# Block products of an MLP down-projection: their weights prepared in three parts, and one weight chunk of the last stage scheduled sooner

## The chip, the cores and the metric

The kernel runs on one core of a Trainium2 chip. The metric is the device time of one execution in microseconds (us), as the median of several executions. A profile is one execution recorded by the hardware. Its engines are TensorE (PE: matmuls; PEld: its weight loads), VectorE (DVE), ScalarE (ACT), GpSimd (POOL) and SyncE (SP, which only issues DMAs here). Each engine works through its own queue of instructions in order, and semaphores make one engine wait for another.

## The reference

Two layers of a decoder trunk over 512 tokens and 1024 features, all in float32. Each layer has a mixer (attention and convolution in layer 0, gated linear attention in layer 1), a gated MLP with a short convolution, and a gated per-layer embedding:

```python
def _conv_ffn(h, w_up, conv_w, conv_b, w_down):
    u = _causal_depthwise_conv(h @ w_up, conv_w) + conv_b
    gate, up = jnp.split(u, 2, axis=-1)
    return (jax.nn.gelu(gate, approximate=False) * up) @ w_down

def _per_layer_embedding(x, p_i, norm, w_gate, w_proj):
    gate = jax.nn.sigmoid(_rms_norm(x, norm) @ w_gate)
    return gate * (p_i @ w_proj)
...
        x = x + _conv_ffn(_rms_norm(x, ffn_norm[i]), ffn_w_up[i], ffn_conv_w[i], ffn_conv_b[i], ffn_w_down[i])
        x = x + _per_layer_embedding(x, p[i], ple_norm[i], ple_w_gate[i], ple_w_proj[i])
```

`w_down` is 2816 x 1024 per layer. This change touches the product with it, in both layers, and the last stage, which is the per-layer embedding of layer 1.

## The kernel before

**Three matmuls for one.** Every float32 operand is split into a high part (a rounded copy, made by ACT: `wh` of a weight) and a low part (the rest, made by DVE: `wl = raw - wh`). A product is then three matmuls: high by high, high by low, low by high. So each chunk of weights passes through ACT and then DVE before PE can use it. Lines 138 and 139 do this for ordinary weights, 811 and 812 (`cut_blocks`) for the weights of block products, 1335 and 1336 (`chunk`) in the last stage.

**Block products.** A part of the weights is multiplied by Strassen's scheme in Winograd's form: seven products of half-sized blocks in place of eight. It needs sums and differences of the four weight blocks b11, b12, b21, b22, which `seven_forms` makes in place with four DVE subtractions (lines 831, 832, 834, 836), and of the activations. From the blocks come four sets of split weights: `plain` (before any subtraction), `t13` (after the first two subtractions, a full chunk from `ev`), `t2` (after the third, half a chunk) and `last` (after the fourth, made in `seven` itself). `seven` is a generator: each `next` emits one group of products. The first is `plain` by tokens into W, which ACT copies into the two result banks X and Y (lines 865 and 866). The second group begins with `t13` into V, then a `plain` and a `t2` product; the third and fourth use `t13` and `last`. V is added to both halves of the odd output row at the end (line 1237, the V add).

**The down-projection.** `down` works on four units of 256 output columns. Rows A and B of `w_down` are multiplied in the ordinary way, in steps listed in `plan`; rows C, the last eight row blocks, by `seven`, for units 0 to 3 in layer 0 and 0 to 2 in layer 1. A plan entry with a fifth number s carries the block products of unit s interleaved with its own steps. Units 0 and 2 have their C weights in a `raw` tile; units 1 and 3 in two `zt` tiles, loaded as even and odd row blocks, whose `plain` set is made in two halves (lines 102 and 103).

**What sets the order.** PE's order is the order of the program text. DVE's and ACT's are set by a scheduler from the order of the text and its priorities. The split weights `wh` and `wl` have three buffers each. The list `todo` holds the work that needs such buffers, each with the number it needs; `pump(n)` says that n more have come free and takes from the list what fits. An ordinary cut needs one; the preparation of a unit needed two, for `plain` and `t13` together.

**The last stage.** `ple1` multiplies a gate matrix by the same kind of scheme, with PE, DVE and ACT in the written order from line 1418 on. Ahead of that stand two chunks of block (0,0) (`w11`), the subtraction `minus(b11, b12, b11)` in two halves, and `wt1`, the split of its first half, which is the third chunk. `wt1` is used by the s1 products. Between the first six matmuls of these and the rest stand eight sums of squares (line 324) and eight transposes (line 1262); then come the s2 products, transposes (1364) and the projection (lines 158 to 160, with the chunk `wj`).

Of the kernel before, what the change touches and what calls it, by code (L numbers as in the profile page):

```python
# [14 lines left out]
ALU = mybir.AluOpType  # L15
# [42 lines left out]
class Kernel:  # L58
# [758 lines left out]
    def seven_forms(self, ev, od, raw=None):  # L817


        nc = self.nc  # L820
        b11, b12, b21, b22 = ev[:, :, :P], ev[:, :, P:], od[:, :, :P], od[:, :, P:]
        if raw is not None:
            plain = self.cut_blocks(raw[:, :, :P])
        else:
            h, l = (self.wp.tile([P, 1024], F32R, tag=g, name=self.nm(g), bufs=3) for g in ("wh", "wl"))
            h, l = (x.rearrange("p (j u n) -> p j u n", u=2, n=P) for x in (h, l))
            for u, b in enumerate((b11, b21)):
                self.split((h[:, :, u], l[:, :, u]), b)
            plain = lambda j, c: (h[:, j, c], l[:, j, c])

        nc.vector.tensor_tensor(b11, b12, b11, ALU.subtract)
        nc.vector.tensor_tensor(b12, b22, b12, ALU.subtract)  # L832
        t13 = self.cut_blocks(ev)
        nc.vector.tensor_tensor(b11, b22, b11, ALU.subtract)
        t2 = self.cut_blocks(b11, False)
        nc.vector.tensor_tensor(b21, b21, b11, ALU.subtract)
        return plain, t13, t2

    def seven(self, od, ws, xg, forms, keep=True):

# [249 lines left out]
    def down(self, i, acts, forms, both, work, finish):  # L1090


        nc, tc = self.nc, self.tc
        H = S // 2
        wd = self.a["ffn_w_down"][i].rearrange("(k p) n -> p k n", p=P)
        rows = {"A": (8, 14), "B": (0, 8), "C": (14, 22)}

        plan = [(0, "A", 0, 3), (0, "A", 3, 6), (0, "B", 0, 4), (0, "B", 4, 8)]
        plan += [(1, "A", 0, 3), (1, "A", 3, 6), (1, "B", 0, 4), (1, "B", 4, 8, 0)]
        plan += [(2, "B", 0, 4, 1), (2, "B", 4, 8, 2)]  # L1100
        if i == 0:
            plan += [(2, "A", 0, 4, 3), (2, "A", 4, 6), (3, "B", 0, 4), (3, "B", 4, 8), (3, "A", 0, 3), (3, "A", 3, 6)]
            loads = ["A0", "B0", "A1", "B1", "C0", "B2", "C2", "A2", "B3", "A3"]
            inner = ["C1", "C3"]
        else:
            plan += [(2, "A", 0, 3), (2, "A", 3, 6), (3, "B", 0, 4), (3, "B", 4, 8)]
            plan += [(3, "C", 0, 4), (3, "C", 4, 8), (3, "A", 0, 3), (3, "A", 3, 6)]
            loads = ["A0", "B0", "A1", "B1", "C0", "B2", "C2", "A2", "B3", "C3", "A3"]
            inner = ["C1"]
        blocked = 4 - i  # L1110
        plan = [p if len(p) == 5 else p + (None,) for p in plan]
        got, cuts, gens = {}, {}, {}

        def cols(u):
            return slice(2 * P * u, 2 * P * u + 2 * P)

        def load(key):
            k0, k1 = rows[key[0]]
            u = int(key[1])
            raw = self.raw(k1 - k0, 2 * P)  # L1120
            nc.sync.dma_start(raw, wd[:, k0:k1, cols(u)])
            got[key] = (raw, None)

        def load_inner(key):
            k0, k1 = rows[key[0]]
            u = int(key[1])
            parts = []
            for q in range(2):
                t = both().rearrange("p a (b n) -> p (a b) n", n=2 * P)
                nc.sync.dma_start(t, wd[:, k0 + q : k1 : 2, cols(u)])  # L1130
                parts.append(t)
            got[key] = (None, parts)

        def cut(t):
            u, name, k0, k1, _ = plan[t]
            cuts[t] = self.cut(got[f"{name}{u}"][0][:, k0:k1], "a")
            if k1 == rows[name][1] - rows[name][0] and loads:
                load(loads.pop(0))

        def prepare(u):  # L1140
            raw, parts = got[f"C{u}"]
            ev, od = parts or self.by_parity(raw)
            ws = self.seven_forms(ev, od, raw)
            gens[u] = self.seven(od, ws, acts[14:], forms, False)

        def cut_done(u):

            raw, _ = got[f"C{u}"]
            if raw is not None and loads:
                load(loads.pop(0))  # L1150
            elif raw is None and inner:
                load_inner(inner.pop(0))

        todo = []
        for t, p in enumerate(plan):
            todo.append((1, lambda t=t: cut(t)))
            if p[4] is not None:
                todo.append((2, lambda u=p[4]: prepare(u)))
        free = 3

        def pump(n):
            nonlocal free
            free += n
            while todo and todo[0][0] <= free:
                need, f = todo.pop(0)
                free -= need
                f()

        def add(m, ps):
            nc.vector.tensor_tensor(self.xT[m], self.xT[m], ps, ALU.add)  # L1170

        due = [2 if u < blocked else 1 for u in range(4)]
        block_left = blocked
        next_unit = 0

        banks = {}
        with tc.manual_schedule(engines={ET.PE}):
            with tc.high_priority(offset=300):
                for _ in range(2):
                    load(loads.pop(0))  # L1180
                pump(0)
            for t, (u, name, k0, k1, s) in enumerate(plan):
                own = u not in banks
                if own:
                    banks[u] = [self.ps(), self.ps()]
                ends = t + 1 == len(plan) or plan[t + 1][0] != u
                joined = i == 0 and u == 3

                def steps(lo, hi):
                    for k in range(lo, hi):  # L1190
                        for c in range(2):
                            self.mm3(
                                banks[u][c], cuts[t](k, c * P, (c + 1) * P), acts[rows[name][0] + k0 + k],
                                start=own and k == 0, stop=ends and k == k1 - k0 - 1, skip_group_check=joined,
                            )

                def settled(ends):
                    nonlocal next_unit
                    if ends:
                        for c in range(2):  # L1200
                            add(2 * u + c, banks[u][c])
                        due[u] -= 1
                    while not block_left and next_unit < 4 and not due[next_unit]:
                        for m in (2 * next_unit, 2 * next_unit + 1):
                            finish(m)
                        next_unit += 1

                if s is None:
                    steps(0, k1 - k0)
                    settled(ends)  # L1210
                    pump(1)
                    if work:
                        work.pop(0)()
                        if not work:
                            load_inner(inner.pop(0))
                else:
                    g = gens[s]
                    steps(0, 1)
                    next(g)
                    steps(1, 2)  # L1220
                    next(g)
                    steps(2, 3)
                    next(g)
                    cut_done(s)
                    pump(1)
                    steps(3, 4)
                    settled(ends)
                    pump(1)
                    X, Y, V = next(g)
                    if i == 0 and s == 3:  # L1230
                        banks[3] = [X, Y]
                    else:
                        add(2 * s, X)
                        add(2 * s + 1, Y)
                    pump(1)
                    x = self.xT[2 * s + 1].rearrange("p (u t) -> p u t", u=2)
                    nc.vector.tensor_tensor(x, x, V.unsqueeze(1).to_broadcast([P, 2, H]), ALU.add)
                    due[s] -= 1
                    block_left -= 1
                    settled(False)  # L1240
# [69 lines left out]
    def ple1(self, fp):  # L1310
# [31 lines left out]
        def minus(out, x, y):  # L1342
            for q in range(2):
                c = slice(2 * q, 2 * q + 2)
                nc.vector.tensor_tensor(out[:, c, :], x[:, c, :], y[:, c, :], ALU.subtract)
# [65 lines left out]
        proj_load(1)  # L1411
        b21 = block(1, 0, False)
        proj_load(0)
        minus(b11, b12, b11)
        wt1 = [chunk(b11[:, :2, :])]
        X, Q = [[self.ps() for _ in range(2)] for _ in range(2)]
        both = (0, H)
        with tc.manual_schedule(engines={ET.PE, ET.DVE, ET.Activation}):
# [525 lines left out]
```

## Time and profile before

| | us |
|---|---|
| median of 3 runs | 1243.28 (1241.5 to 1243.61) |
| the profiled execution | 1243.01 |
| its span, first to last instruction | 1241.2 |
| PE busy | 1225.9 |
| DVE busy | 920.4 |
| ACT busy | 640.2 |

In a row of the timeline the columns are start and duration in us, engine, line, operation, output and inputs, shape, and count. In square brackets stands the idle time of the engine ahead of the instruction and what ended it. Matmuls overlap in their durations, so the work of PE is read from start to start: a 512-column matmul follows the one before it after about 0.23 us. The down-projection of layer 0 runs from 419 to 538 us, that of layer 1 up to 1176 us, and the last stage from there to the end.

### The profile page before, as it was taken

The page shows a single profiled execution, that of the slowest core. Times are in us where ns is not written, and L with a number is a line of the kernel's source. Part 1 is how long each engine was busy: PE and PEld are TensorE (multiplying, and loading weights), DVE is VectorE, ACT ScalarE, POOL GpSimd, SP SyncE. Part 2 cuts the span into 40 slices and gives each one's busy share as a digit, 9 for nine tenths or more (in the row PEclk, how much of TensorE's full clock was granted, in tenths as well). Part 3 has the DMA queues.
Part 4 walks back from the last instruction along what each step waited for, and adds up shares of the span by engine and source line. Part 5 has one row for each costly group of instructions (what it writes and reads, how often), then busy time and mean ns, then how long its engine had stood idle before and what let it go on. Part 6 is the DMA issues. An engine that isn't in the chain of part 4 may idle for free.

```text
span 1241.2 us, 16978 instructions
## 1 busy us (share of the span) xinstructions
PE 1225.9 (99%) x6740; PEld 1047.2 (84%) x6740; DVE 920.4 (74%) x1449; ACT 640.2 (52%) x1036; POOL 42.7 (3%) x64
## 2 busy tenths in 40 slices
PE   9999999999999999999999999999999999999998
PEld 8877788889999888888978888888889999888877
DVE  6886556987878976745779875559878789968575
ACT  7466343554556743544563544435455557635354
POOL 3500000000000000000100000000000000000000
PEclk9999999999999999999999999999999999999989
DMA  6322232224242432233322212333322423413501
GB/s 215 102 71 61 79 102 79 92 68 136 69 135 70 136 117 68 88 102 100 108 69 68 76 61 70 100 110 102 102 77 69 136 68 128 139 57 117 173 1 68
DMA packets 111060, 117.56 MB, mean 95 GB/s; under 512 B 2777, under 2 KB 106259, under 8 KB 110981
## 3 DMA queue, kind: packets, MB, share of 16 engines
q1 hardware_dynamic: 109616, 115.35, 28.5%
q8 instruction: 53, 0.87, 0.3%
q0 software_dynamic: 560, 0.42, 0.3%
q10 hardware_dynamic: 804, 0.70, 0.2%
q14 instruction: 27, 0.21, 0.1%
HBM read 114.37 MB, written 2.10 MB: 94 GB/s over the span
## 4 chain that ended last, share of the span: by engine, by line
PE 87%; DVE 8%; ACT 3%; issue 2%; POOL 1%; ACTq 0%; DVEq 0%; POOLq 0%
PE ps L158 16%; PE ps L159 16%; PE ps L160 16%; PE pa L159 5%; PE pa L158 5%; PE pa L160 5%; PE ps L854 4%; PE ps L856 4%; PE ps L855 4%; PE pa L856 2%; PE pa L855 2%; PE pa L854 2%; DVE wl L139 1%; PE ps L1357 1%; PE ps L1358 1%
## 5 line engine op out<-in xcount | busy, mean ns | idle before, releaser
L138 ACT ACTIVATE wh<-raw 128x1024 fp32r<-128x1024 f32 (+4 forms) x170 | 169.3, 998 | 225.4 <-PE ps L159 167.9
L139 DVE TENSOR_TENSOR wl<-raw,wh 128x1024 fp32r<-128x1024 f32 (+4 forms) x170 | 194.9, 1147 | 94.6 <-ACT wh L138 94.2
L158 PE MATMUL ps<-a,wh 128*128 128x512 f32 x416 | 162.7, 391 | 0.0
L159 PE MATMUL ps<-a,wh 128*128 128x512 f32 x416 | 162.3, 390 | 0.0
L160 PE MATMUL ps<-a,wl 128*128 128x512 f32 x416 | 162.0, 390 | 0.0
L158 PE MATMUL ps<-b,wh 128*128 128x512 f32 x320 | 126.2, 396 | 0.5 <-ACT b L102 0.5
L160 PE MATMUL ps<-b,wl 128*128 128x512 f32 x320 | 125.7, 393 | 0.0
L159 PE MATMUL ps<-b,wh 128*128 128x512 f32 x320 | 125.2, 392 | 0.0
L811 ACT ACTIVATE wh<-raw 128x1024 fp32r<-128x1024 f32 x54 | 57.1, 1058 | 69.1 <-DVE raw L832 30.1
L158 PEld LDWEIGHTS ps<-a,wh 128*128 128x128 f32 x416 | 78.1, 188 | 16.6 <-issue 0.7
L160 PEld LDWEIGHTS ps<-a,wl 128*128 128x128 f32 x416 | 78.1, 188 | 16.4
L159 PEld LDWEIGHTS ps<-a,wh 128*128 128x128 f32 x416 | 78.2, 188 | 16.2 <-issue 0.3
L158 PE MATMUL pa<-a,wh 128*128 128x512 f32 x224 | 87.8, 392 | 0.0
L159 PE MATMUL pa<-a,wh 128*128 128x512 f32 x224 | 87.8, 392 | 0.0
L160 PE MATMUL pa<-a,wl 128*128 128x512 f32 x224 | 87.1, 389 | 0.0
L812 DVE TENSOR_TENSOR wl<-raw,wh 128x1024 fp32r<-128x1024 f32 x54 | 65.9, 1221 | 28.0 <-ACT wh L811 27.9
L158 PEld LDWEIGHTS ps<-b,wh 128*128 128x128 f32 x320 | 60.1, 188 | 13.5 <-ACT b L102 1.3
L910 DVE SCALAR_TENSOR_TENSOR zt<-z,vfa,zt 128x511 f32<-128x511 f32 (+1 forms) x92 | 67.1, 746 | 5.3 <-ACT zt L908 5.0
L160 PEld LDWEIGHTS ps<-b,wl 128*128 128x128 f32 x320 | 60.1, 188 | 12.7
L159 PEld LDWEIGHTS ps<-b,wh 128*128 128x128 f32 x320 | 60.2, 188 | 11.5
L160 PEld LDWEIGHTS pa<-a,wl 128*128 128x128 f32 x224 | 42.1, 188 | 9.2
L158 PEld LDWEIGHTS pa<-a,wh 128*128 128x128 f32 x224 | 42.3, 189 | 7.3
(460 smaller groups left out, 2945.1 us busy)
## 6 DMA issues: line engine op xcount, KB each, us to landing
raw<-in_ffn_w_up_dram SPq DMA_DIRECT2D x44, 1024.0 KB, 4.9
raw<-in_ffn_w_down_dram SPq DMA_DIRECT2D x13, 1024.0 KB, 5.2
raw<-in_hy_w_in_dram SPq DMA_DIRECT2D x8, 1024.0 KB, 5.0
raw<-in_gla_w_in_dram SPq DMA_DIRECT2D x8, 1024.0 KB, 5.1
raw<-in_ffn_w_down_dram SPq DMA_DIRECT2D x8, 768.0 KB, 4.3
raw<-in_ple_w_gate_dram SPq DMA_DIRECT2D x6, 1024.0 KB, 5.0
raw<-in_gla_w_out_dram SPq DMA_DIRECT2D x4, 1024.0 KB, 4.9
zt<-in_ffn_w_down_dram SPq DMA_DIRECT2D x6, 512.0 KB, 3.7
```

The lines of the kernel that those rows point to most:

```text
L138: nc.scalar.activation(hv, v, AF.Copy)
L139: nc.vector.tensor_tensor(lv, v, hv.bitcast(F32), ALU.subtract)
L158: mm(out, lh, rh, start=start, stop=False, **kw)
L159: mm(out, lh, rl, start=False, stop=False, **kw)
L160: mm(out, ll, rh, start=False, stop=stop, **kw)
L811: nc.scalar.activation(h, src, AF.Copy)
L812: nc.vector.tensor_tensor(l, src, h.bitcast(F32), ALU.subtract)
L854: mm(out, wh, xh, start=first and j == 0, stop=False, **kw)
L855: mm(out, wh, xl, start=False, stop=False, **kw)
L856: mm(out, wl, xh, start=False, stop=j == ND // 2 - 1, **kw)
L910: nc.vector.scalar_tensor_tensor(out=y[:, tap:], in0=z[:, : S - tap], scalar=w[:, f : f + 1], in1=y[:, tap:], op0=ALU.mult, op1=ALU.add,)
L1357: mm(o, lh, rl, start=False, stop=False, **kw)
```

## The change

The preparation of a unit is cut into three. `first_forms` makes `plain` and does the first two subtractions, as soon as one buffer is free. `more_forms` of `down` makes `t13` as soon as the next is free. The rest (third and fourth subtraction and `t2`) is put on a list `pending`, which is worked off after the adds of a unit. In the main loop one `pump(1)` moves ahead of `settled(ends)`, and the V add moves ahead of the adds of X and Y. In `ple1` the subtraction and the third chunk get a higher priority.

```diff
     def seven_forms(self, ev, od, raw=None):
+        plain = self.first_forms(ev, od, raw)
+        return plain, self.cut_blocks(ev), self.more_forms(ev, od)
+
+    def first_forms(self, ev, od, raw=None):
...
         nc.vector.tensor_tensor(b11, b12, b11, ALU.subtract)
         nc.vector.tensor_tensor(b12, b22, b12, ALU.subtract)
-        t13 = self.cut_blocks(ev)
+        return plain
+
+    def more_forms(self, ev, od):
+        nc = self.nc
+        b11, b21, b22 = ev[:, :, :P], od[:, :, :P], od[:, :, P:]
         nc.vector.tensor_tensor(b11, b22, b11, ALU.subtract)
         t2 = self.cut_blocks(b11, False)
         nc.vector.tensor_tensor(b21, b21, b11, ALU.subtract)
-        return plain, t13, t2
+        return t2
...
+        def pend():
+            while pending:
+                pending.pop(0)()
...
-        def prepare(u):
+        def first_forms(u):
             raw, parts = got[f"C{u}"]
             ev, od = parts or self.by_parity(raw)
-            ws = self.seven_forms(ev, od, raw)
-            gens[u] = self.seven(od, ws, acts[14:], forms, False)
+            gens[u] = ev, od, self.first_forms(ev, od, raw)
+
+        def more_forms(u):
+            ev, od, plain = gens[u]
+            t13 = self.cut_blocks(ev)
+
+            def rest():
+                gens[u] = self.seven(od, (plain, t13, self.more_forms(ev, od)), acts[14:], forms, False)
+
+            pending.append(rest)
...
             if p[4] is not None:
-                todo.append((2, lambda u=p[4]: prepare(u)))
+                todo.append((1, lambda u=p[4]: first_forms(u)))
+                todo.append((1, lambda u=p[4]: more_forms(u)))
...
                     steps(0, k1 - k0)
                     settled(ends)
                     pump(1)
+                    pend()
...
                     steps(3, 4)
+                    pump(1)
                     settled(ends)
+                    X, Y, V = next(g)
                     pump(1)
-                    X, Y, V = next(g)
+                    x = self.xT[2 * s + 1].rearrange("p (u t) -> p u t", u=2)
+                    nc.vector.tensor_tensor(x, x, V.unsqueeze(1).to_broadcast([P, 2, H]), ALU.add)
                     if i == 0 and s == 3:
                         banks[3] = [X, Y]
                     else:
                         add(2 * s, X)
                         add(2 * s + 1, Y)
-                    pump(1)
-                    x = self.xT[2 * s + 1].rearrange("p (u t) -> p u t", u=2)
-                    nc.vector.tensor_tensor(x, x, V.unsqueeze(1).to_broadcast([P, 2, H]), ALU.add)
+                    pend()
...
         proj_load(0)
-        minus(b11, b12, b11)
-        wt1 = [chunk(b11[:, :2, :])]
+        with tc.high_priority(offset=150):
+            minus(b11, b12, b11)
+            wt1 = [chunk(b11[:, :2, :])]
```

More of the change, by code (lines that the diff above doesn't have):

```diff
@@ L1111, in down @@
         plan = [p if len(p) == 5 else p + (None,) for p in plan]
-        got, cuts, gens = {}, {}, {}
+        got, cuts, gens, pending = {}, {}, {}, []
+        def pend():
+            while pending:
+                pending.pop(0)()
         def cols(u):
```

## The prediction

> **What bounds the kernel now.** I read the page's shares first, then the slices, then the waits of the matmul engine, and last the timelines of the stages that the diff touches.
>
> ```profile
> span 1241.2 us, 16978 instructions
> PE 1225.9 (99%) x6740; PEld 1047.2 (84%) x6740; DVE 920.4 (74%) x1449; ACT 640.2 (52%) x1036; POOL 42.7 (3%) x64
> PEclk9999999999999999999999999999999999999989
> ```
>
> TensorE is the bound from end to end. So the change can gain only what TensorE loses now: idle time in front of matmuls, and time at a lower clock. All slices show 9 for the granted clock except the last but one. The waits of PE in the whole span name the lines of this change:
>
> ```profile
> PE ps L1357 <- DVE wl L1336: 2.2, 1, 2.2
> PE pa L856 <- DVE wl L812: 1.5, 2, 0.8
> PE pa L854 <- ACT wh L811: 0.7, 2, 0.4
> ```
>
> Columns are total us, times, and the longest. The first is the largest single wait of PE in the kernel: one wait of 2.2 us in the last stage. The other two are the block products of the down-projection: two waits each, one in each layer's down-projection. The clock goes with the first one:
>
> ```profile
> 1185.30:1192.10 6.80, 6.80 (x26) 6.02 (x25) 3.99 (x6) 3.95 (x6) 1.01 (x1) 0.50 0.00 0
> ```
>
> This is the view by stretches; the third figure from the end is the granted clock, 0.50 for 6.8 us.
>
> **The change, part by part.** Three things move; the instructions stay the same in number and kind (one merged pair of DVE subtractions is now split in order). The orders of DMA issues on SP, of POOL, and of PE's products are as before, so no transfer and no product is moved.
>
> *1. The t13 weights of unit 1 (both layers).* PE in the first down-projection:
>
> ```profile
> 471.48 0.39 PE L160 MATMUL ps<-b,wl 128*128 128x512 f32 x1
> 472.23 0.39 PE L854 MATMUL pa<-a,wh 128*128 128x256 f32 x1 [0.36 <-ACT wh L811]
> 472.45 0.28 PE L855 MATMUL pa<-a,wh 128*128 128x256 f32 x1
> 473.49 0.38 PE L856 MATMUL pa<-a,wl 128*128 128x256 f32 x1 [0.75 <-DVE wl L812]
> 473.71 0.28 PE L854 MATMUL pa<-a,wh 128*128 128x256 f32 x1
> 473.83 0.28 PE L855 MATMUL pa<-a,wh 128*128 128x256 f32 x1
> ```
>
> ```profile
> 465.64 1.38 DVE L1170 TENSOR_TENSOR xT<-xT,ps 128x512 f32<-128x512 f32 x2
> 468.90 0.69 DVE L831 TENSOR_TENSOR zt<-zt 128x512 f32<-128x512 f32 x1
> 469.51 0.68 DVE L1237 TENSOR_TENSOR xT<-xT,pa 128x512 f32<-128x512 f32 x1
> 470.10 0.69 DVE L832 TENSOR_TENSOR zt<-zt,zt 128x512 f32<-128x512 f32 x1
> 472.21 1.23 DVE L812 TENSOR_TENSOR wl<-zt,wh 128x1024 fp32r<-128x1024 f32 x1 [1.42 <-ACT wh L811]
> 477.44 1.23 DVE L812 TENSOR_TENSOR wl<-zt,wh 128x1024 fp32r<-128x1024 f32 x1 [1.88 <-ACT wh L811]
> 470.57 0.36 ACT L865 COPY ps<-pa 128x256 f32<-128x256 f32 x1 [1.52 <-PE pa L856]
> 471.10 1.07 ACT L811 ACTIVATE wh<-zt 128x1024 fp32r<-128x1024 f32 x1
> ```
>
> A 256-wide matmul starts 0.12 us after the one before (473.71 to 473.83); a 512-wide one takes 0.23 (below). So the loss at this place is 0.75 - 0.23 = 0.52 in front of wh, 1.04 - 0.12 = 0.92 in front of wl, and 0.10 twice where the first matmul after a wait spaces 0.22: 1.64 us. The cause stands on DVE and ACT. Between 465.64 and the second subtraction (470.10) DVE runs eight half-width steps, 0.60 apart: two adds, half of plain, an add, the other half, subtraction, V add, subtraction. Then ACT does its square and the two copies out of PSUM, which wait for PE until 470.57, and only then wh.
>
> In the new order five steps are left: two halves of plain, subtraction, one add, subtraction. The second subtraction starts at 465.64 + 4 x 0.60 = 468.04 and ends at 468.73. ACT takes wh next, ahead of the square and the copies: 468.8 to 469.9. DVE does two adds meanwhile and then wl, 470.0 to 471.2. PE wants wh at 471.48 + 0.23 = 471.71 and wl 0.24 later at 471.95. Both are there, wl with 0.75 to spare, and ACT is done with wh before the copies' PE product ends at 470.57, so they are not held. Gain 1.64 here. The waits view counts two of each wait with equal longest values, so the second layer's unit 1 is taken as the same: 3.28 together. Bounds: 0 where wl comes no sooner, 3.28 where it comes in time; I take 3.28, since the margin of 0.75 is more than one DVE step.
>
> The V add goes to after t2 and before the last chunk's wl. That wl has 1.88 us of DVE idle ahead of it (477.44), which covers one step of 0.60; without that cover it would cost those 0.60 in each unit's last product. The rest (t2 and the second pair of subtractions) falls behind the adds, but t2 feeds the fourth product, 24 matmuls of 0.12 behind the first of t13: 2.9 us later. Units 0, 2 and 3 show no such wait on PE now, and there only the V add changes its place: 0.
>
> *2. The third chunk of the last stage.*
>
> ```profile
> 1175.88 1.06 ACT L1335 ACTIVATE four<-raw 128x1024 fp32r<-128x1024 f32 x1 [2.55 <-DVE raw L1345]
> 1179.94 1.04 ACT L1335 ACTIVATE wh<-raw 128x1024 fp32r<-128x1024 f32 x1
> 1177.17 1.22 DVE L1336 TENSOR_TENSOR four<-raw,four 128x1024 fp32r<-128x1024 f32 x1
> 1178.41 0.43 DVE L103 TENSOR_TENSOR b<-zt,b 128x256 fp32r<-128x256 f32 x1
> 1181.30 0.69 DVE L280 TENSOR_TENSOR acc<-acc,sq 128x512 f32<-128x512 f32 x1
> 1183.11 1.23 DVE L1336 TENSOR_TENSOR wl<-raw,wh 128x1024 fp32r<-128x1024 f32 x1
> ```
>
> ```profile
> 1181.81 0.39 PE L1356 MATMUL ps<-wh,a 128*128 128x512 f32 x1
> 1184.39 0.50 PE L1357 MATMUL ps<-wl,a 128*128 128x512 f32 x1 [2.19 <-DVE wl L1336]
> 1185.91 1.70 PE L324 MATMUL pa<-ones,acc 128*128 128x1 f32 x8
> 1194.72 0.39 PE L1356 MATMUL ps<-four,a 128*128 128x512 f32 x1
> 1197.45 1.04 PE L1364 MATMUL pa<-cf,xT 128*128 128x128 f32 x8
> 1198.24 0.47 PE L1356 MATMUL ps<-four,b 128*128 128x512 f32 x1
> 1201.32 0.39 PE L159 MATMUL pa<-wl,four 128*128 128x512 f32 x1
> 542.28 1.05 PE L324 MATMUL pa<-ones,acc 128*128 128x1 f32 x8
> 543.20 0.48 PE L158 MATMUL ps<-a,wh 128*128 128x512 f32 x1
> ```
>
> ACT's conversion goes from 1179.94 to right behind the one at 1175.88, so 1176.84 to 1177.9; DVE's goes from 1183.11 to right behind 1177.17, so 1178.3 to 1179.5. PE wants wl at 1181.81 + 0.23 = 1182.04: the wait goes. What DVE and ACT did in between comes 1.1 us later. The low part of the last pair (1178.41) ends at about 1179.9; PE wants that pair six matmuls ahead of 1181.81, at 1180.45. The sum of squares ended at 1181.30 + 0.69 = 1181.99; it goes to 1182.8, since one subtraction of 0.3 now stands behind it. PE wants it six matmuls after 1181.81, at 1183.17: covered, by 0.4 us alone.
>
> From 1181.81 to the s2 products at 1194.72 are 12.91 us. At full clock and without a wait: 24 matmuls at (1197.45 - 1194.72)/12 = 0.2275, so 5.46; eight sums at 543.20 - 542.28 = 0.92; eight transposes at 1198.24 - 1197.45 = 0.79; 0.08 for the slower start behind them. That is 7.25, a gain of 5.66: 2.45 of it is the wait with its slower start, 3.2 is the half clock.
>
> That the half clock goes too is my choice. It is the only one inside the span's stages, it begins 0.9 us after the only wait over 2 us ends, and the 1.6 us lost in the down-projections, spread over two waits, brought none. Bounds: 2.45 (the clock dip stays) and 5.66.
>
> *3. What is late next.* PE comes sooner to the projection, whose weight chunk wj is behind a long DVE chain:
>
> ```profile
> 1187.64 0.16 DVE L167 TENSOR_SCALAR rs<-pa 128x4 f32<-128x4 f32 x1 [0.92 <-PE pa L324]
> 1189.70 2.36 DVE L1336 TENSOR_TENSOR four<-raw,four 128x1024 fp32r<-128x1024 f32 x2 [1.90 <-ACT four L1335]
> 1196.50 2.36 DVE L1336 TENSOR_TENSOR wl<-raw,wh 128x1024 fp32r<-128x1024 f32 x2 [0.97 <-ACT wh L1335]
> 1198.78 1.22 DVE L1336 TENSOR_TENSOR wl<-four,wh 128x1024 fp32r<-128x1024 f32 x1
> ```
>
> wj's wl ends at 1200.00. Moving the third chunk ahead takes nothing off this chain, it only reorders it; sooner it gets by its idle time, 0.92 + 1.90 + 0.97 = 3.79, all of it behind PE or behind ACT copies that wait for PE. If all goes, wj is there at 1196.2; PE wants it at 1201.32 - 5.66 = 1195.66. A new wait of 0.55, with its restart 0.65. Bounds: 0, and 4.4 where none of the idle time goes. I take 0.65, since all three waits end with PE work that comes 2.5 us or more sooner. Gain of the stage: 5.0.
>
> **Sum.** 3.28 + 5.0 = 8.3 us. The profiled execution took 1243.01 us (1.8 beside its span), 0.27 under the median 1243.28 of the runs shown. 1243.0 - 8.3 = 1234.7.
>
> [...]
>
> **The rivals.**
>
> The clock dip stays, for it comes from the eight sums and eight transposes (some 1.7 us of thin work on PE), or moves to another place. For it: that thin work stays and follows more closely. Against: the eight sums at 542.28 brought no dip, and the clock fell at 1185.3, ahead of the sums at 1185.91. PE then reaches wj late enough for no wait: gain 3.28 + 2.45 = 5.7, time 1237.3.
>
> wj does not come sooner, and takes the place of the wait removed. For it: DVE is full in this stretch. Against: the three idle stretches above. Gain 3.28 + 5.66 - 4.4 = 4.5: 1238.5.
>
> The change does not do what it says for unit 1: wl comes late still, for instance because wh finds no free buffer. Against: the buffer it gets was last read by unit 0's last product, over before wh's new start. Gain 5.0 alone: 1238.0.
>
> The new order costs the five units that do not wait now. At 1.2 us in each, 6 of the 8.3 are gone: 1241, no measurable change. For it: every unit's V add is moved. Against: the 1.88 us of idle DVE time.
>
> Slower: a clock that does not recover. If the thin work that now follows closely lets the clock fall and it stays at 0.50, each us at half clock costs 0.5. To end 2.5 us above 1243 it must take 10.8 us back, 22 us at half clock from the sums on, three times the dip seen: 1246. Against: the clock came back at 1192 under ordinary matmuls.
>
> **How the numbers follow.** Forecast 0.60, own range 1233.2 to 1236; dip stays 0.16; wj late 0.08; unit 1 unhelped 0.06; five units hurt 0.06; clock lost 0.04. The low end is the sum without the wj wait (1234.1) less about 1 us, since the three runs shown lie 2.1 us apart. The high end 1239.0 takes in the first three rivals. 0.2% (2.5 us) is about what can be told from no change: faster 0.90, same 0.06, slower 0.04.
>
> **What would show it.** In the waits of PE: no DVE wl of the last stage's s1 products, no wh and wl of t13 in the pa products; granted clock 1.00 from the start of the last stage to its final products; the eight sums in about 0.9 us; a short new PE wait (about 0.5) in front of the projection for wj. I am wrong if PE waits for acc at the sums, if a stretch at 0.50 is left there, or if DVE's V add shows up as what a last chunk waits for.

## The result, and the profile after

The changed kernel takes 1234.78 us (median of 6 runs, 1234.57 to 1235.43). The kernel before, in the 6 runs beside it, takes 1241.83 (1240.62 to 1243.61). The ratio is 0.9943, with a 95% interval of 0.993 to 0.9955. The profiled execution took 1235.43 us, 7.58 less than the profiled one of before.

The page of the changed kernel, its span, busy time and granted clock in 40 slices:

```profile
span 1233.7 us, 16975 instructions
PE 1222.7 (99%) x6740; PEld 1045.2 (85%) x6740; DVE 920.2 (75%) x1449; ACT 640.7 (52%) x1036; POOL 43.6 (4%) x64
PEclk9999999999999999999999999999999999999999
```

The work is the same; the 8 in the clock's last slice but one is gone. The waits of PE in the whole span (total us, times, longest):

```profile
PE pa L1649 <- DVE F L1647: 1.5, 2, 1.0
PE pa L1723 <- ACT qT L1715: 1.3, 2, 0.7
PE pa L193 <- DVE mhalf L182: 1.3, 1, 1.3
PE pa L600 <- ACT pT L654: 1.0, 1, 1.0
PE ps L158 <- ACT b L102: 0.5, 1, 0.5
PE pa L159 <- DVE wl L139: 0.2, 1, 0.2
PE pa L1780 <- ACT vt L1544: 0.2, 1, 0.2
```

These seven stood in the view of before too. The three that named the lines of the change are gone, and no new one is long enough to appear. (Lines have moved: 811 and 812 keep their numbers, the V add is 1255, the block products 863 to 865, the last stage's chunks 1359 and 1360, its products 1380 to 1382.)

Where the time went is read from PE instructions that both programs have, the first of them the first transposes of the kernel. Before:

```profile
9.10 1.04 PE L478 MATMUL ps<-cf,xin 128*128 128x128 f32 x8
464.17 0.39 PE L160 MATMUL ps<-b,wl 128*128 128x512 f32 x1
1203.81 0.39 PE L1356 MATMUL ps<-wh,a 128*128 128x512 f32 x1
```

After:

```profile
10.05 1.04 PE L478 MATMUL ps<-cf,xin 128*128 128x128 f32 x8
465.17 0.39 PE L160 MATMUL ps<-b,wl 128*128 128x512 f32 x1
541.75 1.05 PE L324 MATMUL pa<-ones,acc 128*128 128x1 f32 x8
1179.57 0.39 PE L1380 MATMUL ps<-wh,a 128*128 128x512 f32 x1
1196.24 0.39 PE L1380 MATMUL ps<-wh,a 128*128 128x512 f32 x1
```

The other two starts of before stand in the prediction: eight sums at 542.28 and first s1 product at 1181.81. They give:

| stretch | before | after | gain |
|---|---|---|---|
| up to unit 1 of layer 0's down-projection | 464.17 | 465.17 | -1.00 |
| from there to the eight sums of layer 0's last stage | 78.11 | 76.58 | 1.53 |
| from there to the s1 products of layer 1's last stage | 639.53 | 637.82 | 1.71 |
| s1 products to s3 products | 22.00 | 16.67 | 5.33 |

The gains add up to 8.57. The execution profiled after began 1.0 us later, which leaves 7.57. 0.95 of it is there at the first transposes, long before the change; the kernel of the third experiment, which is that of before up to the last stage, reaches that stage 0.8 us later than the profiled execution of before (1182.61 in a row below, against 1181.81). So this offset belongs to the execution. The traces show where it comes from. The list of clock stretches has the first one at full clock begin 4.32 us after the first instruction in the profiled execution of before and 7.04 in that after the change; for the third experiment it is an estimate, about 7.5, since its eight 512-column matmuls from 6.44 us on take 2.40 where those of after take 2.19 from 6.43 on. Ahead of that rise the first 512-column matmuls start about 0.44 us apart, later 0.23. The later the rise in these three, the later the first transposes: 9.10, 10.05 and 10.27 us.

The down-projection of layer 0, DVE and ACT around unit 1's `t13`:

```profile
469.05 0.69 DVE L836 TENSOR_TENSOR zt<-zt,zt 128x512 f32<-128x512 f32 x1
470.93 1.23 DVE L812 TENSOR_TENSOR wl<-zt,wh 128x1024 fp32r<-128x1024 f32 x1
474.44 0.69 DVE L1255 TENSOR_TENSOR xT<-xT,pa 128x512 f32<-128x512 f32 x1 [0.17 <-PE pa L865]
476.91 1.22 DVE L812 TENSOR_TENSOR wl<-zt,wh 128x1024 fp32r<-128x1024 f32 x1 [1.77 <-ACT wh L811]
```

```profile
469.83 1.06 ACT L811 ACTIVATE wh<-zt 128x1024 fp32r<-128x1024 f32 x1 [3.28 <-DVE zt L836]
471.62 0.36 ACT L874 COPY ps<-pa 128x256 f32<-128x256 f32 x1 [0.21 <-PE pa L865]
```

and PE there:

```profile
472.58 0.39 PE L160 MATMUL ps<-b,wl 128*128 128x512 f32 x1
472.81 0.28 PE L863 MATMUL pa<-a,wh 128*128 128x256 f32 x1
472.93 0.28 PE L864 MATMUL pa<-a,wh 128*128 128x256 f32 x1
473.04 0.28 PE L865 MATMUL pa<-a,wl 128*128 128x256 f32 x1
```

ACT takes `wh` before the copies out of PSUM, not behind them, and PE goes into the block products without a gap.

The last stage on PE:

```profile
1180.93 0.95 PE L324 MATMUL pa<-ones,acc 128*128 128x1 f32 x8
1181.74 1.07 PE L1286 MATMUL pa<-cf,pin 128*128 128x128 f32 x8
1186.76 0.39 PE L1380 MATMUL ps<-four,a 128*128 128x512 f32 x1
1193.10 0.39 PE L158 MATMUL pa<-wh,four 128*128 128x512 f32 x1
1193.61 0.50 PE L159 MATMUL pa<-wl,four 128*128 128x512 f32 x1
1193.95 0.40 PE L160 MATMUL pa<-wh,four 128*128 128x512 f32 x1
```

and on DVE, the third chunk (first row), the sum of squares that PE needs, and the chain to `wj` (last row):

```profile
1176.07 1.22 DVE L1360 TENSOR_TENSOR wl<-raw,wh 128x1024 fp32r<-128x1024 f32 x1
1179.76 0.68 DVE L280 TENSOR_TENSOR acc<-acc,sq 128x512 f32<-128x512 f32 x1
1184.24 2.37 DVE L1360 TENSOR_TENSOR four<-raw,four 128x1024 fp32r<-128x1024 f32 x2
1190.06 2.36 DVE L1360 TENSOR_TENSOR wl<-raw,wh 128x1024 fp32r<-128x1024 f32 x2
1192.34 1.22 DVE L1360 TENSOR_TENSOR wl<-four,wh 128x1024 fp32r<-128x1024 f32 x1
```

The brackets with idle time that stood in these rows of before are gone: from the third chunk to `wj` DVE runs without a stop. By stretches (the third figure from the end is the granted clock), from the s1 products to the s2 products and on:

```profile
1179.50:1186.80 7.30, 7.30 (x43) 6.29 (x42) 7.30 (x12) 5.81 (x9) 1.85 (x1) 1.00 0.00 0
1186.80:1200.00 13.20, 13.07 (x62) 10.61 (x61) 11.67 (x12) 8.93 (x13) 0.00 (x0) 1.00 0.01 1
```

One more thing has to be known to read the runs. Executions of the kernel before differ in their mean granted clock, and the time follows it. The 29 beside the first four experiments fall into three groups: 1.000 (6 runs, 1240.5 to 1241.0 us), 0.998 (10 runs, 1241.7 to 1242.7) and 0.997 (13 runs, 1242.9 to 1243.7). The profiled one, at 0.997, has 6.8 us at half clock, which is 0.5 x 6.8 / 1241 = 0.003 of the span. Half that stretch is 0.0014. So the groups are read as no, one and two such halves; of two the profile of before is the example, of one that of the first experiment below. By this the dip is there in most executions and not in all.

### The profile page after: what moved, and what is told of

The parts are those of the page before. It is cut to its first block, busy times and chain, and to the rows that moved or that the text cites. A ratio compares the mean times of both kernels' runs of the same rounds, so it can differ in the third digit from the quotient of the medians.

```text
span 1233.7 us, 16975 instructions
## 1 busy us (share of the span) xinstructions
PE 1222.7 (99%) x6740; PEld 1045.2 (85%) x6740; DVE 920.2 (75%) x1449; ACT 640.7 (52%) x1036; POOL 43.6 (4%) x64
## 4 chain that ended last, share of the span: by engine, by line
PE 86%; DVE 9%; ACT 2%; issue 2%; POOL 1%; DMA 0%; ACTq 0%; DVEq 0%; POOLq 0%
PE ps L158 16%; PE ps L159 16%; PE ps L160 16%; PE pa L159 5%; PE pa L158 5%; PE pa L160 5%; PE ps L863 4%; PE ps L865 4%; PE ps L864 4%; PE pa L865 2%; PE pa L864 2%; PE pa L863 2%; DVE wl L139 1%; PE ps L1382 1%; PE ps L1381 1%
```

## The experiments

**The down-projection alone.** The changed kernel with the last part taken back:

```diff
-        with tc.high_priority(offset=150):
-            minus(b11, b12, b11)
-            wt1 = [chunk(b11[:, :2, :])]
+        minus(b11, b12, b11)
+        wt1 = [chunk(b11[:, :2, :])]
```

> The change without its part in the last stage. Theory (the two parts add up, each removes its own waits of PE): the waits for t13 in the pa products are gone in both layers, the 2.2 us wait for wl and the half clock of 6.8 us stay; 3.1 us faster than before (0.25%). Rival (the gain hangs on the phase of the clock, not on the waits): the half clock goes here too, since everything comes 3 us sooner; 6 us or more faster.

Measured: 1239.58 us (11 runs, 1237.57 to 1240.11) against 1242.30 for the 29 of before, ratio 0.9975 (0.9966 to 0.9984). Groups of equal mean clock compare better: 1237.6 against 1240.5 to 1241.0 at 1.000, 1238.4 to 1238.8 against 1241.7 to 1242.7 at 0.998, 1239.6 to 1240.1 against 1242.9 to 1243.7 at 0.997. Between the middle runs of these groups lie 3.1, 3.4 and 3.3 us, and 3.28 was predicted. The waits for `t13` are gone, the wait of the last stage stays, and behind it the half clock, about 3.4 us long this time:

```profile
PE ps L1381 <- DVE wl L1360: 2.2, 1, 2.2
```

```profile
1178.00:1183.00 5.00, 2.82 (x14) 2.00 (x12) 4.97 (x8) 1.36 (x3) 0.00 (x0) 1.00 0.00 0
1183.00:1186.40 3.40, 3.40 (x19) 3.30 (x18) 1.28 (x3) 2.15 (x4) 1.01 (x1) 0.57 0.00 0
1186.40:1200.00 13.60, 13.60 (x65) 11.29 (x64) 10.69 (x11) 9.98 (x14) 0.00 (x0) 0.98 0.00 1
```

The length is an estimate from these rows and from matmul starts: a mean clock of 0.57 over 3.40 us is 2.9 us at 0.50, and these are the last of them, from about 1183.5; and the starts at 1186.25, 1186.67, 1187.00 and 1187.23 are 0.42, 0.33 and 0.23 apart, so it is back at about 1186.9.

**The last stage alone.** The kernel before with only that part:

```diff
-        minus(b11, b12, b11)
-        wt1 = [chunk(b11[:, :2, :])]
+        with tc.high_priority(offset=150):
+            minus(b11, b12, b11)
+            wt1 = [chunk(b11[:, :2, :])]
```

> The last stage's part alone. Theory: the waits for t13 stay (1.5 and 0.7 us), the 2.2 us wait and the half clock are gone, a wait of about 0.3 us for the projection's chunk comes; 5.2 us faster than before in an execution that had the half clock. Rival (the half clock comes from the sums and transposes): the clock still falls, only 2.4 us faster.

Measured: 1238.28 (7 runs, 1237.75 to 1239.53), ratio 0.9969 (0.9959 to 0.998). All seven have a mean clock of 0.999 or more, and no half clock shows in the profiled one's last stage. Against before's runs at 0.997 (middle 1243.2) that is 4.9 less, where 5.0 was predicted; against those at 1.000 (middle 1240.7) it is 2.5. The waits of the block products are still in its view:

```profile
PE pa L856 <- DVE wl L812: 1.5, 2, 0.8
PE pa L854 <- ACT wh L811: 0.7, 2, 0.4
```

The two halves gain 2.7 and 4.0 in medians, 6.7 together. The whole change gains 7.05 against the six runs of before beside it, and 7.5 against these 29. With runs of before that spread over 3 us, this shows no sign that the halves disturb each other.

**Is it the idle time, or the thin work?** The kernel before, with matmuls that nobody reads put where PE idles 2.2 us. The wait stays covered, the weights come when they came, and the sums and transposes stay:

```diff
+            self.nowhere = self.pa()
+            self.idle(10)
             add(None, "s1", wt1, first=True, order=steps[:2])
```

> The kernel before, with ten matmuls of ones into an unused bank ahead of the s1 products, so that PE works through most of the 2.2 us in which it waited. The wait is not shorter. Theory (idle PE makes the clock fall): granted clock 1.00 through the stage, 3.2 us faster than before. Rival (the thin work of the sums and transposes makes it fall): 0.50 for 6.8 us as before, no change in time.

Measured: 1240.69 (11 runs, 1239.82 to 1240.86), ratio 0.9988 (0.9979 to 0.9997). So the kernel before becomes a little faster, 1.6 us in the median, by doing more work. PE, and the clock from the first of the ten matmuls on:

```profile
1182.61 2.43 PE L193 MATMUL pa<-ones_r 128*128 128x512 f32 x10
1184.88 0.39 PE L1356 MATMUL ps<-wh,a 128*128 128x512 f32 x1
```

```profile
1182.60:1190.00 7.40, 7.40 (x41) 6.15 (x40) 5.47 (x8) 2.82 (x5) 1.01 (x1) 1.00 0.00 0
```

No half clock in the profiled execution, and ten of the eleven runs are at a mean clock of 1.000 (the other, at 0.999, is the fastest). Its s3 products start at 1201.50, 18.89 after the ten matmuls' start; before they start 22.00 after the same place. The 3.1 of difference is what the dip cost in the profiled execution of before. In medians it comes out smaller: the groups at 0.997 and 1.000 are 2.4 us apart.

**How much idle time?** The same with five matmuls, which leave about half of the wait:

```diff
+            self.nowhere = self.pa()
+            self.idle(5)
```

> The same with five matmuls: about 1.1 us of PE's wait are filled and 1.1 to 1.3 us stay idle, about as much as the two waits of a down-projection together, behind which the clock did not fall. Theory (it takes about 2 us of idle PE close together): clock 1.00, 3.2 us faster. Rival (any idle time right ahead of the thin sums and transposes is enough): 0.50 for 6.8 us, no change.

Measured: 1240.48 (10 runs, 1239.91 to 1242.31), ratio 0.9991 (0.9982 to 1.0). Seven runs are at a mean clock of 0.999 or 1.000 (1239.9 to 1240.9), three at 0.998 (1242.0 to 1242.3). The wait left is

```profile
PE ps L1357 <- DVE wl L1336: 1.0, 1, 1.0
```

So, by the mean clock, a gap of 1.0 us brings the dip in 3 executions of 10, one of 2.2 us in 23 of 29. Neither text on record holds: about 2 us of idle time are not needed in every execution, and any idle time is not enough. In these runs the length of the gap alone does not decide; the last section takes this up.

**The V add back in its old place in the text.** The changed kernel, with

```diff
-                    x = self.xT[2 * s + 1].rearrange("p (u t) -> p u t", u=2)
-                    nc.vector.tensor_tensor(x, x, V.unsqueeze(1).to_broadcast([P, 2, H]), ALU.add)
                     if i == 0 and s == 3:
                         banks[3] = [X, Y]
                     else:
                         add(2 * s, X)
                         add(2 * s + 1, Y)
+                    x = self.xT[2 * s + 1].rearrange("p (u t) -> p u t", u=2)
+                    nc.vector.tensor_tensor(x, x, V.unsqueeze(1).to_broadcast([P, 2, H]), ALU.add)
```

> The changed kernel with the V add back behind the adds of X and Y. Theory (what counts is that ACT makes t13's high part ahead of its PSUM copies; the V add was covered): the same time as the changed kernel within 0.3 us, no wait of PE for wh or wl in the block products. Rival (the V add between the two subtractions was the delay): the wait for wl comes back, up to 0.6 us in each layer.

Measured: 1234.82 (4 runs, 1234.28 to 1234.88), the changed kernel's time, and no wait for `t13`. So the place of the V add in the text does not matter. The rival is not tested by this, because the scheduler did not put the add back between the two subtractions, where it stood at 469.51 before: here it runs at 471.78, behind `wl` of `t13`. An estimate from the rows of the changed kernel: a step of 0.60 between the subtractions would fit into the 0.9 us by which `wl` is early. That the earlier place of `t13` is what counts is read from the rows; no run takes it back alone.

**More thin work.** The changed kernel with more transposes into unread banks, behind the eight of the last stage:

```diff
+            for _ in range(2):
+                more = self.pa()
+                for t in range(NT):
+                    nc.tensor.transpose(more[:, t * P : (t + 1) * P], pin[0][:, t, :], self.ident)
             add(None, "s1", wt1, order=steps[2:])
```

> The changed kernel with sixteen more transposes, whose results nobody reads, behind the eight of the last stage; the thin stretch on PE grows from 1.6 to about 3.2 us, without a wait. Theory (PE's clock falls after a stretch in which the array moves little, waiting or not): the clock falls to 0.50 for some 6.8 us; 1.6 + 3.4 = 5 us slower than the changed kernel. Rival (only waits count): clock 1.00, 1.6 us slower.

The text on record speaks of sixteen; the kernel has eight (two times `NT`, which is 4). Measured: 1235.69 (4 runs, 1235.63 to 1235.81), 0.9 above the changed kernel, which is the eight transposes' own time at about 0.1 each, with runs 0.2 us apart. Eight are short against the stretches seen, so the loop was set to sixteen:

```diff
-            for _ in range(2):
+            for _ in range(16):
```

> The changed kernel with sixty-four more transposes of 128 x 128 (into banks that nobody reads) behind the eight transposes in front of the rest of the s1 products; nothing is left out. At 0.1 us each they make the thin work on the matmul engine, with the eight sums and the eight transposes, 8 us without a gap. If only idle time lets the clock fall: no stretch at half clock, 6.4 us more than the changed kernel less the wait for wj of 0.4: 1240.8. If transposes count as idle for the clock: one or two stretches of 3.4 us at 0.50 behind them, which take 1.7 to 3.4 us more: 1242.5 to 1244.2.

Measured: 1242.50 (10 runs, 1242.07 to 1242.80), 7.7 above the changed kernel where 6.0 was expected. No wait for `wj` is left, and the clock does not fall in the profiled execution; the ten lie within 0.7 us, less than a dip costs:

```profile
1182.26 8.27 PE L1459 MATMUL pa<-cf,pin 128*128 128x128 f32 x64
1190.28 0.47 PE L1380 MATMUL ps<-wh,a 128*128 128x512 f32 x1
```

```profile
1180.50:1190.30 9.80, 9.56 (x82) 8.58 (x81) 9.18 (x11) 4.61 (x7) 1.85 (x1) 1.00 0.01 2
1190.30:1200.00 9.70, 9.70 (x50) 8.11 (x48) 3.50 (x3) 4.99 (x7) 0.00 (x0) 1.00 0.00 0
```

The 64 take 8.02 us from start to start and not 6.4; 1.2 of the excess are four waits of about 0.3, for banks still in use, as the view of the tile `pin` lists them:

```profile
  PE pa L1459: 1.2, 4
```

That was the error of the expectation. The time would also fit the other expectation, 1242.5 to 1244.2 with a dip, but the clock in the rows decides against it. In this place almost 10 us without a wide matmul, at a clock of 1.00, did not lower the clock by themselves. Whether it can prolong a dip that a wait has begun is not tested.

**What is still lost.** Two steps beyond the change. First, the copy out of PSUM from ACT to DVE in `seven`, which takes away short waits of the block products; then also `wj` cut ahead of a subtraction and two chunks that are needed later:

```diff
-        nc.scalar.copy(Y[:, right], X[:, right])
+        (nc.scalar.copy if keep else nc.vector.tensor_copy)(Y[:, right], X[:, right])
```

> The changed kernel with the copy of X's right half to Y in the down-projection on DVE, since on ACT it stands behind a 1.06 us conversion and PE then starts the next product 0.2 us late, in five units that the timeline shows. Theory: these waits go, 1 us faster than the changed kernel. Rival: DVE is no sooner there, since its own work for the unit stands ahead of the copy; no change or slower.

```diff
             add(None, "s1", wt1, order=steps[2:])
+            wj = chunk(wj_raw[:, 2:, :])
             minus(b12, b22, b12)
             kd = keep(Q, "R")
             wt3 = chunks(b12)
-            wj = chunk(wj_raw[:, 2:, :])
```

> The same, and the projection's chunk wj is prepared ahead of the two wt3 chunks in the last stage. Theory: PE's wait of 0.3 us (0.4 with its restart) for wj goes and wt3 is still in time, since its products follow 2.7 us later; 0.4 us faster than with the copy on DVE alone, 1.4 us faster than the changed kernel. Rival: wt3 becomes late by its 1.1 us; slower by up to 0.7 us.

Measured: 1234.08 with the copy (5 runs, 1233.77 to 1234.48, ratio 0.9933) and 1233.67 with both (5 runs, 1233.09 to 1234.26, ratio 0.9929, 0.9917 to 0.9942). The copy brings 0.7 where 1 was expected; in unit 1 of layer 0 a new wait of similar length stands a little later:

```profile
467.90 0.39 PE L160 MATMUL ps<-b,wl 128*128 128x512 f32 x1
468.35 0.50 PE L158 MATMUL ps<-b,wh 128*128 128x512 f32 x1
```

The version with `wj` too is 0.4 lower in the median, the length of its wait, which is gone from the profile; the runs of the two overlap, so the times alone do not show it. The version with both is below both kernels, though against the changed one by 1.1 us only.

## Why the prediction was right

**Step 1, the t13 weights.** It was worked out in the time of before; 1.0 us is added here. The second subtraction was to start at 469.04 and did at 469.05; ACT's `wh` at 469.8 and did at 469.83; DVE's `wl` at 471.0 and did at 470.93. It ends at 472.16, and PE comes to it at 473.04, with 0.9 to spare (0.75 predicted). Predicted gain 1.64 in each layer, 3.28; measured 1.53 and 1.71 over the two stretches, 3.24 (the second stretch holds more than the down-projection).

**The V add at nothing.** Right: the last chunk's `wl` still has 1.77 us of idle DVE in front of it (1.88 before), and moving the add back in the text changes nothing.

**Step 2, the third chunk.** From the s1 to the s2 products 7.25 us were predicted and 1186.76 - 1179.57 = 7.19 measured. The sums wanted `acc` at 1180.93 and it was there at 1180.44: a margin of 0.5 (0.4 predicted). That the half clock would go with the wait was the one choice in it, and the experiment with ten matmuls shows it: the wait covered, everything else left, no dip. 3.2 us were put down for the dip, and the profiles show 3.1. In the profile of before a wait of 2.19 us went ahead of 6.8 us at 0.50.

**Step 3, the wait for wj.** Predicted 0.65, measured 0.39: from 1193.10 to 1193.61 are 0.51, which is 0.28 over the usual spacing of 0.23, and 0.11 for the slower start behind it. The mechanism held, and the size was a little less: all three stretches of idle DVE went, as predicted, and `wj` was ready 13.99 after the first s1 product, where 14.4 was predicted.

**The sum.** Predicted 8.3, measured 8.57 between the two profiles, less 1.0 by which this execution began later. That the median, 1234.78, lies within 0.1 us of the forecast 1234.7 is in part luck: between the two profiles the terms gained 0.3 more than forecast, and the later start of 1.0, which the prediction did not have, took more than that back. The difference of medians also agrees less well: 7.05 where 8.3 was forecast.

**What the prediction did not see.** It took the half clock of the profiled execution as a part of every execution. It is one of three cases. The gain is 8.4 us against the runs of before at a mean clock of 0.997 (middle 1243.2), 6.0 against those at 1.000 (1240.7), and 7.05 between the medians of the six runs each. After the change the runs lie within 0.9 us; before they spread over 3.

**The rivals.** The dip did not stay. `wj` came sooner. Unit 1 was helped. The other units lost nothing that shows: the two down-projections' stretches give 3.24 of 3.28. The clock stayed at 1.00 under the thin work, and under almost six times as much (9.8 us in the profile with 64 more transposes).

## What to carry to other kernels

A wait of the bounding engine can cost more than its length (here 2.19 us of wait went with 3.1 us for the dip behind it): look at the granted clock by stretches right behind each long wait, and price the dip with the wait. The cheapest test of it is to fill the gap with work that nobody reads, and see whether the kernel becomes faster. Where a dip sits in a profile, look at the mean clock of all runs first, since a single profile may show the worst case of several.

When a weight chunk is late, ask which operations stand ahead of it in the queue without being needed sooner. Here the order of a few operations alone, with nothing added or taken away, gave the whole gain.

## What the runs showed that was not expected

The half clock differs in length between executions, behind waits of nearly the same length. In the profile of before it lasts 6.8 us behind a wait of 2.19; in that of the first experiment it lasts about 3.4 us behind one of 2.18. It begins 0.9 us behind the end of the wait in the one, and about 1.8 us behind it in the other. The stretch of before that holds the wait is still at 1.00:

```profile
1181.92:1185.33 3.41, 1.22 (x6) 0.81 (x5) 3.38 (x5) 0.13 (x1) 0.00 (x0) 1.00 0.00 0
```

With five matmuls in the gap 1.05 us of wait were left, and the profiled execution shows no dip behind them.

What decides whether a wait brings a dip, and how long the dip is, was not shown. The runs of one kernel fall into groups by their mean clock though the program is the same (no dip in 6 of 29 runs of before, by the reading above), and no run tells what sets the groups apart.

That the groups at 0.997 and 1.000 are 2.4 us apart, while the profiles show 3.1 for the dip, fits the later start: the profiled execution of the third experiment was 0.8 us later ahead of the last stage, and 3.1 - 0.8 = 2.3. No execution of before without a dip was profiled, so this is only argued.

The transposes did not lower the clock: 64 of them in a row over 8.0 us, behind eight sums and eight transposes, left it at 1.00 in the profiled execution.
